# Transposing an 8192 x 8192 matrix: two load slots in place of three

## The chip, the cores and the metric

One core of a Trainium2 chip runs the kernel. The metric is the device time of one execution in microseconds (us); lower is better. Where several runs are shown, their median counts.

## The reference

```python
def setup_inputs():
    return {
        "x": np.random.randn(8192, 8192).astype(np.float32),
    }

def reference(x: np.ndarray) -> np.ndarray:
    return np.transpose(x)
```

The input and the output are 268 MB each, in HBM. Nothing is calculated; every element has to be read once, brought to another place and written once.

## The kernel before, in words

**Chunks.** The input is cut into chunks of 128 rows and 4096 columns, 2 MB each. There are two column halves of 64 row blocks, so 128 chunks; chunk t is row block t mod 64 of half t div 64. One step of the kernel is one chunk. A load (L100) brings a chunk into one of three slots `ins` of 16 KB per partition: chunk t goes to slot t mod 3.

**TensorE.** `transposes` (L109) waits until the slot's load has landed, and then transposes the chunk in 32 pieces of 128 x 128 through a multiplication with `ident` (L117), eight to each of four groups of PSUM banks. After each group it raises `s_pe` (L122). The loop of L132 runs on TensorE alone: its body is three steps, the slots 2, 0, 1, and slot 2 is skipped in the first turn, since 128 is not a multiple of three.

**Evictions.** Group h of a step (h = 0 to 3) is copied from PSUM to SBUF by ScalarE if h is even and by VectorE if it is odd (L208), once `s_pe` says that TensorE has done with it. A group holds two strips q = 2h and 2h + 1 of 512 columns each. A strip gathers eight consecutive chunks in a region of SBUF, 2 MB, before it is stored, so that rows of up to 1024 elements (4 KB) are written to the output. There are nine regions for the eight strips; a strip that begins a new region takes the one that has been free longest, and its eviction waits until that region's last store has landed (L189).

**Stores.** The strips are staggered: strip q is complete in steps with t mod 8 = q. So each step issues one store of 2 MB, after the eviction that completes it, which is in group h = (t mod 8) div 2: the first group in steps 0 and 1 of eight, the fourth in steps 6 and 7. At the beginning the regions hold fewer chunks and the stores are smaller (256 KB for the first), at the end all eight strips are stored in the last step. Where a strip runs over from one column half to the other, its store is split in two.

**Order.** All stores (L28, L160) and all loads but the first ones are issued by ScalarE's queue, ACT. Its program is written out step by step: the step's two evictions, the store at the place where the strip closes, then a wait until TensorE has done with the whole chunk (L223), then the load of the chunk that will use the same slot (L224). So the DMA queue of ACT receives stores and loads in turn. The first loads, one for each slot, are issued by SyncE (SP) at once. SP's last work is to wait for all stores (L226).

Of the kernel before, what the change touches and what calls it, by code (L numbers as in the profile page):

```python
# [40 lines left out]
def kernel(  # L41
# [12 lines left out]
    nc = tc.nc  # L54
    P = 128
# [5 lines left out]
    B = 4  # L61
    W = 8
    NR = S // B
    NIN = 3
    NREG = 9
    CH = N // P
    J = S * P

    with tc.tile_critical():  # L69
        nc.alloc_sbuf_tensor("pad", [P, 32], dt)  # L70
        ident = nc.alloc_sbuf_tensor("ident", [P, P], dt).ap()
        ins = [nc.alloc_sbuf_tensor(f"in{k}", [P, J], dt).ap() for k in range(NIN)]
        SIZE = B * W * P
# [3 lines left out]
        s_id = nc.alloc_semaphore("s_id")  # L77
        s_ld = [nc.alloc_semaphore(f"s_ld{k}") for k in range(NIN)]
        s_st = [nc.alloc_semaphore(f"s_st{k}") for k in range(NREG)]
        s_bank = [nc.alloc_semaphore("s_banka"), nc.alloc_semaphore("s_bankv")]  # L80
        s_pe = nc.alloc_semaphore("s_pe")
        s_cp = [nc.alloc_semaphore("s_cpa"), nc.alloc_semaphore("s_cpv")]

# [3 lines left out]
            out=ident,  # L87
            in_=ident,
# [6 lines left out]

        chunks = [(s, c) for s in range(M // J) for c in range(CH)]

        def load(t):
            s, c = chunks[t]
            (nc.sync if t < NIN else nc.scalar).dma_start(  # L100
                out=ins[t % NIN], in_=x[c * P:(c + 1) * P, s * J:(s + 1) * J]
            ).then_inc(s_ld[t % NIN], 16)

# [3 lines left out]
        def transposes(k):  # L109
            nc.tensor.sem_inc(s_ld[k], -16).wait_op(s_ld[k], 16, "sem-ge")  # L110
            for h in range(NR // 2):
                if h < 2:
                    n = NR // 4
                    nc.tensor.sem_inc(s_bank[h], -n).wait_op(s_bank[h], n, "sem-ge")  # L114
                for b in range(2 * B):
                    j = (2 * h + b // B) * B * P + b % B
                    tr = nc.tensor.transpose(  # L117
                        pss[h][:, b * P:(b + 1) * P],
                        ins[k][:, j:j + B * P - B + 1:B],
                        ident,  # L120
                    )
                tr.then_inc(s_pe, 1)  # L122

        T = len(chunks)
        assert T % NIN == NIN - 1
        pe = [nc.tensor.engine]
        for e in range(2):
            nc.tensor.sem_inc(s_bank[e], NR // 4)  # L130
        nc.tensor.wait_ge(s_id, 2)
        with nc.Fori(0, T // NIN + 1, engines=pe) as turn:  # L132
            with nc.tensor.If(turn > 0):
                transposes(NIN - 1)
            for k in range(NIN - 1):
                transposes(k)

        for t in range(NIN):
            load(t)
# [6 lines left out]
        def store(q, e, count):  # L146
            t0, r, parts = window.pop(q)
            nc.scalar.wait_ge(s_cp[e], count)
            base = 0
            for s, a, z in parts:  # L150
                rows = (z - a) * P
                j0 = s * J + q * B * P
                dst = out[j0:j0 + B * P, a * P:a * P + rows]
                dst = dst.rearrange("(q b) i -> q b i", q=P)
                src = regs[:, r * SIZE + base:r * SIZE + base + B * rows]
                base += B * rows
                if any(stored):
                    st = wide_dma(nc, nc.scalar, "qActDynamicHW", dst, src)
                else:
                    st = nc.scalar.dma_start(  # L160
                        out=dst, in_=src.rearrange("q (b i) -> q b i", b=B)
                    )
                st.then_inc(s_st[r], 16)
                stored[r] += 1
            free.append(r)

        def closes(w, t):
            t0, r, parts = w
            return t + 1 == t0 + sum(z - a for _, a, z in parts)

        for t, (s, c) in enumerate(chunks):
            for h in range(NR // 2):
                e = h % 2
                eng = (nc.scalar, nc.vector)[e]

                place = []
                for q in (2 * h, 2 * h + 1):
                    if q not in window:

                        span = (q - c) % W + 1
                        r = free.pop(0)
                        parts = [(s, c, min(c + span, CH))]
                        if c + span > CH and t + span < T:
                            parts.append((s + 1, 0, c + span - CH))
                        window[q] = (t, r, parts)
                        if stored[r]:
                            eng.wait_ge(s_st[r], 16 * stored[r])  # L189
                    t0, r, parts = window[q]  # L190
                    k = [p[0] for p in parts].index(s)
                    base = r * SIZE + B * P * sum(z - a for _, a, z in parts[:k])
                    _, a, z = parts[k]
                    place.append((base + (c - a) * P, (z - a) * P))
                ends = [q for q in (2 * h, 2 * h + 1) if closes(window[q], t)]
                gap = place[1][0] - place[0][0]
                runs = [(0, 1)]
                if place[0][1] != place[1][1] or abs(gap) >= 2 ** 15:
                    runs = [(0,), (1,)]
                eng.wait_ge(s_pe, t * NR // 2 + h + 1)  # L200
                closing = []
                for u in runs:
                    off, dist = place[u[0]]
                    dims = [list(regs.ap[0]), [gap, len(u)], [dist, B], [1, P]]
                    o = bass.AP(regs.tensor, regs.offset + off, dims)
                    i = pss[h][:, u[0] * B * P:(u[-1] + 1) * B * P]
                    i = i.rearrange("p (l b i) -> p l b i", b=B, i=P)
                    cp = nc.scalar.copy(out=o, in_=i) if e == 0 else nc.vector.tensor_copy(out=o, in_=i)  # L208
                    mine = [q for q in ends if q - 2 * h in u]
                    if mine:  # L210
                        cp.then_inc(s_cp[e], 1)
                        copied[e] += 1
                        closing += [(q, e, copied[e]) for q in mine]
                    if u is runs[-1]:
                        if mine:
                            eng.wait_ge(s_cp[e], copied[e])
                            eng.sem_inc(s_bank[e], 1)
                        else:
                            cp.then_inc(s_bank[e], 1)
                for k in closing:  # L220
                    store(*k)
            if t + NIN < T:
                nc.scalar.wait_ge(s_pe, (t + 1) * NR // 2)  # L223
                load(t + NIN)  # L224
        for r in range(NREG):
# [31 lines left out]
```

## Time and profile before

| what | value |
|---|---|
| median of three runs | 1264.52 us (1263.98 to 1265.18) |
| the profiled execution's own time | 1265.02 us |
| its span, first to last instruction | 1262.9 us |
| TensorE busy with matmuls | 742.7 us (59%) |
| VectorE busy | 316.1 us (25%) |
| ScalarE busy | 263.0 us (21%) |
| bytes moved by DMA | 536.98 MB, mean 425 GB/s |
| packets of ACT's queue, share of all DMA bytes | 98.8% |
| mean granted TensorE clock | 0.749 |

The profile is one execution, taken by the hardware profiler. TensorE's busy time sums matmuls that overlap with weight loads, so it says little of how much TensorE could do[...]. "DMA" in the slices is the mean busy share of the core's 16 DMA engines. For an issue of a DMA the page gives the median time from issue to landing, which includes the time that the transfer stands in the queue. The granted clock tells how much TensorE was throttled; one step's 32 matmuls take between 4.1 us (full clock, at the beginning) and 6.7 us.

### The profile page before, as it was taken

Reading aid. Unit: us, or ns where it says so; the run is one execution under the profiler, and the core shown is the slowest. Engines: PE = TensorE matmul, PEld = TensorE weight load, DVE = VectorE, ACT = ScalarE, POOL = GpSimd, SP = SyncE. Lnnn points to the kernel's source line nnn. Section 1 sums busy time; section 2 is a strip of 40 time slices with the busy share of each in tenths; the row PEclk is TensorE's granted clock in tenths of the full one; section 3 lists DMA queues with packets and bytes.
Section 4 is the critical chain, followed back from the end, with each engine's and each line's share of the span. In section 5 each row is a group of like instructions: output and inputs, shape, how many; then the busy total and the mean of one; then the engine's idle time right before and its main releaser. Section 6 shows DMA issues by size and latency. Waiting matters only on the chain. (4 is left out here: it accounts for less than half of the span.)

```text
span 1262.9 us, 9961 instructions
## 1 busy us (share of the span) xinstructions
PE 742.7 (59%) x4096; PEld 721.8 (57%) x4096; DVE 316.1 (25%) x311; ACT 263.0 (21%) x321; POOL 0.7 (0%) x6
## 2 busy tenths in 40 slices
PE   6565565665566555655566655666565655656561
PEld 5565555665566555655565655656565645655561
DVE  3322222222222222222222222222222222222220
ACT  3212121222122211212221121121212211122120
POOL 0000000000000000000000000000000000000000
PEclk9967768677777777686766687777868687777865
DMA  9999999999999999999999999999999999999998
GB/s 381 429 430 420 429 431 428 430 429 431 428 430 430 431 428 429 430 430 430 426 425 414 429 430 429 430 430 430 428 430 430 431 428 430 430 430 429 430 427 339
DMA packets 39274, 536.98 MB, mean 425 GB/s; under 512 B 4320, under 2 KB 4832, under 8 KB 6240
## 3 DMA queue, kind: packets, MB, share of 16 engines
q10 hardware_dynamic: 38832, 530.60, 98.8%
q1 hardware_dynamic: 432, 6.29, 1.2%
q14 instruction: 9, 0.07, 0.0%
q8 instruction: 1, 0.02, 0.0%
HBM read 268.44 MB, written 268.44 MB: 425 GB/s over the span
## 5 line engine op out<-in xcount | busy, mean ns | idle before, releaser
L117 PE MATMUL ps<-ident,in 128*128 128x128 f32 x4096 | 742.7, 364 | 493.1 <-PEq L114 493.1
L117 PEld LDWEIGHTS ps<-ident,in 128*128 128x128 f32 x4096 | 721.8, 219 | 513.9 <-issue 513.6
L208 DVE COPY regs<-ps 128x1024 f32<-128x1024 f32 (+1 forms) x311 | 316.1, 1034 | 921.2 <-PE ps L117 704.5
L208 ACT COPY regs<-ps 128x1024 f32<-128x1024 f32 (+1 forms) x320 | 261.7, 843 | 973.6 <-PE ps L117 654.9
L208 ACT ACT_TABLE_LOAD x1 | 1.3, 1283 | 0.9 <-SPq L69 0.9
L86 POOL TENSOR_SCALAR_AFFINE_SELECT ident<-ident 128x128 f32<-128x128 f32 x1 | 0.3, 293 | 0.2 <-POOL ident L84 0.2
L84 POOL MEMSET ident<- 128x128 f32 x1 | 0.2, 204 | 0.5 <-SPq L69 0.5
L241 POOL MEMSET const-bfloat16-1.0<- 128x1 bf16 x1 | 0.1, 102 | 0.0
L241 POOL MEMSET const-uint8-127<- 128x1 uint8 x1 | 0.1, 102 | 0.0
L241 POOL MEMSET const-float32-0.0<- 128x1 f32 x1 | 0.1, 99 | 0.2 <-issue 0.2
L241 POOL MEMSET const-float32-1.0<- 128x1 f32 x1 | 0.1, 99 | 0.0
## 6 DMA issues: line engine op xcount, KB each, us to landing
in<-in_x_dram ACTq DMA_DIRECT2D x125, 2048.0 KB, 22.5
out_dram<-regs ACTq DMA_DIRECT2D x114, 2048.0 KB, 18.4
out_dram<-regs ACTq DMA_DIRECT2D x4, 1792.0 KB, 17.5
in<-in_x_dram SPq DMA_DIRECT2D x3, 2048.0 KB, 11.6
out_dram<-regs ACTq DMA_DIRECT2D x4, 1536.0 KB, 15.1
out_dram<-regs ACTq DMA_DIRECT2D x4, 1280.0 KB, 16.7
out_dram<-regs ACTq DMA_DIRECT2D x4, 1024.0 KB, 16.6
out_dram<-regs ACTq DMA_DIRECT2D x4, 768.0 KB, 16.4
```

The lines of the kernel that those rows point to most:

```text
L84: nc.gpsimd.memset(ident, 0.0).then_inc(s_id, 1)
L86: nc.gpsimd.affine_select(out=ident, in_=ident, compare_op=mybir.AluOpType.not_equal, fill=1.0, base=0, pattern=[[-1, P]], channel_multipl ...
L117: tr = nc.tensor.transpose(pss[h][:, b * P:(b + 1) * P], ins[k][:, j:j + B * P - B + 1:B], ident,)
L208: cp = nc.scalar.copy(out=o, in_=i) if e == 0 else nc.vector.tensor_copy(out=o, in_=i)
L241: nc = _bacc.Bacc("TRN2", target_bir_lowering=False, num_devices=1)
```

## The change

There are two slots in place of three, so chunk t goes to slot t mod 2, and the load that ACT issues after step t is that of chunk t + 2 in place of t + 3. SP issues two loads at the beginning in place of three. TensorE's loop has two steps in its body and runs 64 turns, with no branch in it. The 16 KB of SBUF per partition that the third slot held stay unused; the regions, the evictions and the stores are as before.

The first load into a slot that has been used, that of chunk 2, is issued in two halves of 2048 columns: the first half after TensorE has done with the first two groups of chunk 0, the second after all four. Both raise a semaphore of their own, `s_half`. VectorE waits for both after its evictions of chunk 1 and then raises the semaphore of slot 0 by 16, for which TensorE waits. From chunk 3 on loads are issued whole, at the place in ACT's program where they stood.

```diff
-    NIN = 3
+    NIN = 2
...
+        s_half = nc.alloc_semaphore("s_half")
...
-        def load(t):
+        def load(t, part=None):
             s, c = chunks[t]
+            j0, j1 = (0, J) if part is None else (part * J // 2, (part + 1) * J // 2)
             (nc.sync if t < NIN else nc.scalar).dma_start(
-                out=ins[t % NIN], in_=x[c * P:(c + 1) * P, s * J:(s + 1) * J]
-            ).then_inc(s_ld[t % NIN], 16)
+                out=ins[t % NIN][:, j0:j1], in_=x[c * P:(c + 1) * P, s * J + j0:s * J + j1]
+            ).then_inc(s_ld[t % NIN] if part is None else s_half, 16)
...
-        assert T % NIN == NIN - 1
-        pe = [nc.tensor.engine]
+        assert T % NIN == 0
...
-        with nc.Fori(0, T // NIN + 1, engines=pe) as turn:
-            with nc.tensor.If(turn > 0):
-                transposes(NIN - 1)
-            for k in range(NIN - 1):
+        with nc.Fori(0, T // NIN, engines=[nc.tensor.engine]):
+            for k in range(NIN):
                 transposes(k)
...
                 for k in closing:
                     store(*k)
-            if t + NIN < T:
+
+                if t == 0 and h % 2:
+                    nc.scalar.wait_ge(s_pe, h + 1)
+                    load(NIN, h // 2)
+            if t == NIN - 1:
+                nc.vector.wait_ge(s_half, 32)
+                nc.vector.sem_inc(s_ld[0], 16)
+            if 0 < t < T - NIN:
                 nc.scalar.wait_ge(s_pe, (t + 1) * NR // 2)
                 load(t + NIN)
```

## The prediction

> **What bounds the kernel now.** I read the page's slices first, then the waits, the DMA issues, the timeline of the last full rounds, and the table of stretches. The slices say which resource is full:
>
> ```profile
> DMA  9999999999999999999999999999999999999998
> GB/s 381 429 430 420 429 431 428 430 429 431 428 430 430 431 428 429 430 430 430 426 425 414 429 430 429 430 430 430 428 430 430 431 428 430 430 430 429 430 427 339
> ```
>
> The DMA engines are busy in every slice and move about 430 GB/s in nearly all of them. 536.9 MB at 430 GB/s is 1248.6 us of a span of 1262.9 us; the 14 us left are the first slice (381), the last (339) and small dips. So a change helps only by making a transfer faster or filling a hole, and hurts by opening a hole. The waits and issues say how far the queue is ahead:
>
> ```profile
> DVE regs L208 <- PE ps L117: 704.5, 201, 12.2
> PEld ps L117 <- issue: 513.6, 128, 8.4
> ACT regs L208 <- DMA out_dram<-regs: 260.3, 45, 9.2
> DVE regs L208 <- DMA out_dram<-regs: 214.8, 30, 7.9
> ...
> in<-in_x_dram ACTq DMA_DIRECT2D x125, 2048.0 KB, 22.5
> out_dram<-regs ACTq DMA_DIRECT2D x114, 2048.0 KB, 18.4
> ```
>
> TensorE waits 128 times, once per chunk, for a load (513.6 us; 4.0 us a chunk). The evictions wait for TensorE and, 75 times, for a store to free a region. A load lands 22.5 us after its issue though it takes 2.1 MB / 430 GB/s = 4.88 us: it stands behind three to four others in one queue. That cover is what the change spends. One round and what comes after it, steps 125 to 127 (5, 6 and 7 of their group of eight):
>
> ```profile
> 1209.66 6.27 PE L117 MATMUL ps<-ident,in 128*128 128x128 f32 x32 [3.70 <-PEq L114]
> ...
> 1219.42 6.47 PE L117 MATMUL ps<-ident,in 128*128 128x128 f32 x32 [3.50 <-PEq L114]
> ...
> 1225.93 1.22 DVE L208 COPY regs<-ps 128x1024 f32<-128x1024 f32 x1 [1.52 <-PE ps L117]
> 1227.19 0.55 ACTq L28 DMA_DIRECT2D out_dram<-regs  x1
> ```
>
> A step lasts 1219.42 - 1209.66 = 9.76 us, two transfers of 4.88. TensorE needs P = 6.47 us of it (5.2 to 6.7 over the run, with the clock). Last, whether all DMA engines are equally far:
>
> ```profile
> 120.00:640.00 520.00, 309.75 (x1696) 301.19 (x1696) 132.13 (x133) 108.06 (x128) 0.00 (x0) 0.75 1.01 429
> 640.00:690.00 50.00, 31.09 (x160) 30.28 (x160) 12.57 (x15) 10.31 (x13) 0.00 (x0) 0.67 1.01 417
> ...
> 1256.00:1258.00 2.00, 0.00 (x0) 0.00 (x0) 0.00 (x0) 0.00 (x0) 0.00 (x0) 0.50 0.49 208
> 1258.00:1262.00 4.00, 0.00 (x0) 0.00 (x0) 0.00 (x0) 0.00 (x0) 0.00 (x0) 0.50 0.10 41
> ```
>
> The last two numbers of a row are DMA share and GB/s. At the end most engines stop near 1256.7 us and one or two go on to 1261.2: the slowest is some 4.5 us behind. The landing records say the same of the middle: the last of a load's 16 engines lands 3.6 us after the first at 300 us and 5.5 us at 1100 us.
>
> **What the Trainium skill says.** "DMA: Bandwidth & Descriptors", section Bandwidth, puts the ceiling at 435 GB/s (16 ports); the trace's 430 agrees, so no gain in rate is to be had. The same page, section Latency and other measured facts, gives about 0.6 us to the first byte for a DMA issued from SP or ACT; the trace has 1.0 us from the start of the first load's issue (0.94) to its first packet (1.94), with 0.37 us of issue in it. "Trainium Kernel Development and Optimization", Best Practices, asks for double buffering to overlap DMA with compute; the change is just that depth, and whether two are enough is the sum below.
>
> **Part 1: two slots, steady state.** Load t+2 is now issued when TensorE has done with chunk t; before, it was load t+3. The queue's order becomes load t, store t-1, load t+1, store t, load t+2. Count from L, when load t lands on the slowest engine. The landing comes about 0.4 us after the last packet (load 0: packets end at 7.54 to 7.83, landings 7.85 to 8.17). After L the queue still holds store t-1 and load t+1: cover to L + 9.76 - 0.4 = L + 9.36.
> What must arrive by then is store t. It comes latest in steps 6 and 7 of eight, where it follows the fourth eviction: load 126 lands at 1219.13 (0.29 ahead of the matmuls), the store is issued at 1227.19, L + 8.06 = P + 1.59. From issue to first packet take 1.3 us: at 1227.19 some engines had run dry and their next packets begin at 1228.4 to 1228.6. So the need is P + 2.9, met while P is below 6.46. The larger P of each of the 16 pairs of steps 6 and 7 is between 5.56 and 6.68; four exceed 6.46, by 0.02, 0.19, 0.03 and 0.22. A hole in step 6 lengthens the cover of step 7, so a pair counts once: +0.5 us. Other end: if the first packet pays the latency that load 0's first packets showed (1.36 against 611 ns, 0.75 more), the bound is P below 5.71 and the same sum over the pairs is 6.8 us; low end 0. I take 0.5, since the packets after the dry spot took the usual 611 ns.
> In the other six steps the store is issued at L + 3.4 to about L + 6.8, and the load after it at P + 0.3 (L + 6.8 at most), behind that store's 4.88 us: nothing.
>
> **Part 2: the engines lose their lead.** A fast engine now runs at most 9.36 - (P + 2.9), about 0 to 0.9 us, ahead of the slowest before it has nothing to do. Before, it could lead by 5 us, so a stall of one engine was absorbed when another was already behind. Summing in the DMA records the packets that took longer than usual, engine by engine: from step 20 on the worst engine loses 3.6 us (the landings: load 20 at 181.11 to load 127 at 1228.89 is 1047.8, less 107 x 9.76 = 1044.3, 3.5 us). With the leads cut back to the slack at each pair, the same stalls sum to about 6.0 us; with no slack at all, and the ramp in it, 10 us more than now. I take +2.5; ends 0 and +10.
>
> **Part 3: the ramp, and the two halves.** Two loads on SP's queue (2 x 0.4 us of issue) end at about 12.6 us in place of three at 17.7. The first half of load 2 is issued once TensorE has done half of chunk 0 (second eviction's start, 12.15), the second after 14.6. Store 0 (11.06 + 1.3 = 12.4) fills in until about 13.4, the first half arrives at 13.2 to 13.9 and takes 2.4 us, the second is there before it ends: a hole of 0 to 0.5. On ACT each half's issue (0.36) stands ahead of an eviction that waits for TensorE anyhow. The new wait on VectorE stands after chunk 1's evictions (end 20.5); nothing is queued behind it but chunk 2's, and TensorE waits for it: chunk 2 starts at about 20.8 against 19.48. Load 3 is issued at 19.2 and flows at 20.2 to 20.6, store 1 having ended at 20.0: another 0.2 to 0.6. From then on a load (4.88) and a growing store cover P of 4.1 us. Against this, the before kernel loses time here too (391 GB/s between 20 and 26 us, 0.5 us). Ends -0.8 and +1.5; I take +0.5.
>
> **Part 4: at nothing.** TensorE's loop has 64 turns of two steps, in place of 43 of three with a branch; its back edge falls into the 3.3 to 4 us wait for a load (without that cover I see 0.3 us between chunks 1 and 2). The 75 waits for stores (475 us) go: store t-1 lands at L + 4.9, and step t+1, which needs its region, starts at L + 9.76. What is late next there is TensorE, and behind it the load, so nothing is won. In the tail the first two final stores arrive at L + 4.7 with cover to L + 4.5: +0.2; the last bytes are the same.
>
> **Sum.** 0.5 + 2.5 + 0.5 + 0.2 = +3.7 us. The profiled execution took 1265.02 (span 1262.9 and 2.1 around it), so 1268.7 there; the median of the runs is 0.5 lower, 1264.52, so 1268.2.
>
> **The rivals.** *No change to be measured* (within 0.2%, 2.5 us, about what a measurement of this kernel tells from none): stalls seldom hit different engines and the slack holds; parts 1, 2 and 3 at 0.5, 0.5 and 0, about 1265.5. For it: the cover, 9.36, exceeds the need in 12 of 16 pairs.
> *Starved in steps 6 and 7*: the store pays full start latency and the engines go in lockstep. Parts at 5, 6 and 1: about 1276.5, up to 1284. It decides from a lead above 1.3 us. Against it: the packets at 1228.5, which were of normal length.
> *Faster*: the shallower queue ends the clog where stores are split at the middle of the run. There ACT's load issues take 3 to 5 us, the queue having no room, and the rate is 417: 13/430 x 50 = 1.5 us; with the 0.5 at 20 to 26 us and the 0.65 at 104 to 109 (374 GB/s in 5 us), and engines no more behind, -3.5 with nothing lost: 1261. It decides if the rate at that stage reaches 429 and stays 430 elsewhere. Against it: the same slow packets appear at 104 us, where nothing is clogged.
>
> **How the numbers follow.** Forecast (1267 to 1272) 0.45, no change 0.27, starved 0.18, faster 0.10. Range 1263 to 1278: it leaves out most of the faster case and the upper part of the starved one. Slower is 0.45 + 0.18.
>
> **What would show it.** Loads landing about 12 to 13 us after issue, stores near 8 to 10; no evictions waiting for stores; steps of 9.76 us with longer ones where P is above 6.46; DMA share below 1.0 only around steps 6 and 7; a last slice nearer 430, the engines ending together. A step of 10 us or more throughout steps 6 and 7 would make part 1 wrong; a rate above 430, or loads still 20 us in the queue, would overturn all of it.

## The result, and the profile after

| | before | after |
|---|---|---|
| time, median | 1264.06 us (1263.41 to 1265.18, 6 runs) | 1325.52 us (1318.0 to 1332.45, 6 runs) |
| ratio | | 1.0487, 95% interval 1.0442 to 1.0533 |
| profiled execution, own time / span | 1265.02 / 1262.9 us | 1318.0 / 1316.2 us |

The changed kernel is slower by 4.9%, some 61 us, where 3.7 us were forecast and the range ended at 1278. The sign was right, the size was not. The profiled execution of the changed kernel is the fastest of its six, so its trace shows 53 of the 61 us. The slices of the page and its DMA issues, of the changed kernel:

```profile
DMA  8999999999999999999999999999999999999999
GB/s 339 373 403 422 391 427 417 409 425 385 423 392 410 426 414 425 393 415 422 379 420 411 383 417 392 427 424 414 427 396 424 410 410 427 409 427 406 403 426 377
...
in<-in_x_dram ACTq DMA_DIRECT2D x125, 2048.0 KB, 13.5
out_dram<-regs ACTq DMA_DIRECT2D x114, 2048.0 KB, 9.6
```

The DMA engines still read "busy" in nearly every slice, but no slice reaches 430 GB/s and many lie at 380 to 415. So the busy digit hides the loss: the engines have work, and each piece of it takes longer. Landings come 13.5 and 9.6 us after issue in place of the 22.5 and 18.4 us of before. The waits (total us, times, longest us):

```profile
ACT regs L205 <- PE ps L119: 1006.8, 247, 9.1
DVE regs L205 <- PE ps L119: 977.6, 256, 12.2
PEld ps L119 <- issue: 571.5, 128, 8.6
```

The 75 waits of evictions for stores are gone, as forecast, and TensorE waits 571.5 us for loads, 58 us more than before. Cutting both traces where chunk 8's matmuls start (75.35 us, before 63.00) and where TensorE ends says in which stage the time went. The stretches (start and end; length; busy time and count of PE, PEld, DVE, ACT, POOL; clock, DMA share, GB/s), first of before, then of after:

```profile
0.00:63.00 63.00, 36.70 (x257) 35.17 (x257) 20.31 (x27) 18.34 (x31) 0.70 (x6) 0.97 0.98 405
63.00:1236.00 1173.00, 706.03 (x3840) 686.64 (x3840) 294.49 (x283) 243.58 (x288) 0.00 (x0) 0.74 1.01 429
1236.00:1263.00 27.00, 0.00 (x0) 0.00 (x0) 1.27 (x2) 1.07 (x2) 0.00 (x0) 0.55 0.78 324
```

```profile
0.00:75.35 75.35, 39.60 (x256) 38.19 (x257) 20.30 (x27) 18.34 (x31) 0.70 (x6) 0.87 0.94 355
75.35:1293.00 1217.65, 702.38 (x3839) 683.19 (x3840) 295.49 (x282) 244.91 (x288) 0.00 (x0) 0.75 1.00 412
1293.00:1316.00 23.00, 0.29 (x3) 0.10 (x1) 1.29 (x2) 1.07 (x2) 0.00 (x0) 0.55 0.94 390
```

The ramp costs 12.4 us, the 120 steps of the body 45.1 us (10.15 us each in place of 9.77), and the tail gives 4.1 us back: 53.3 us, the difference of the two spans (these figures take TensorE's exact ends, 1235.87 and 1293.29 us; the rows are cut at round times). In the body TensorE's work is the same, the DMA share is 1.00, and the rate is 412 GB/s and not 429. What it looks like from close by, in steps 6 and 7 of a group of eight (chunks 62 and 63), first the timeline (start, length, engine, line, operation; the wait before it in brackets), then stretches of 2 us:

```profile
626.45 5.46 PE L119 MATMUL ps<-ident,in 128*128 128x128 f32 x32 [5.62 <-PEq L116]
...
631.94 1.29 DVE L205 COPY regs<-ps 128x512 f32<-128x512 f32 x2 [0.63 <-PE ps L119]
632.66 0.55 ACTq L28 DMA_DIRECT2D out_dram<-regs  x1
633.25 0.60 ACTq L102 DMA_DIRECT2D in<-in_x_dram  x1
...
636.38 5.56 PE L119 MATMUL ps<-ident,in 128*128 128x128 f32 x32 [4.48 <-PEq L116]
```

```profile
630.00:632.00 2.00, 1.90 (x16) 1.71 (x15) 1.35 (x3) 0.98 (x2) 0.00 (x0) 1.00 1.03 442
632.00:634.00 2.00, 0.00 (x0) 0.00 (x0) 1.23 (x2) 0.10 (x1) 0.00 (x0) 1.00 0.67 287
634.00:636.00 2.00, 0.00 (x0) 0.00 (x0) 0.00 (x0) 0.00 (x0) 0.00 (x0) 1.00 0.96 401
636.00:638.00 2.00, 1.62 (x8) 1.65 (x9) 0.00 (x0) 0.00 (x0) 0.00 (x0) 0.64 1.01 393
638.00:640.00 2.00, 2.00 (x12) 2.00 (x11) 0.00 (x0) 1.07 (x2) 0.00 (x0) 0.51 0.94 279
```

The store is issued at 632.66, 6.5 us behind the landing of its chunk (626.16), when only the load that lands at 636.09 is ahead of it. Most of the engines are through with that load at about 633.1 us and have nothing until 633.9 (share 0.67). That is the hole that the forecast priced. But at 638 to 640 us the share is 0.94 and the rate 279 GB/s: hardly an engine is idle, the packets are long (up to 1.2 us, usually 0.611). Summing the DMA records from 80 us to 10 us before TensorE's end, averaged over the 16 engines: idle 10.0 us (before 0.2), time by which packets ran over their usual length 41.6 us (before 2.5). Four fifths of the loss have no hole at all.

A word on a quantity used below. *Lead* is the landing of the transfer ahead in the queue less the start of the issue, from the DMA records between 100 and 1200 us. *Lag* is how much later the last of the 16 engines lands than the median one. A landing counts for a semaphore only when all 16 engines are through (the Trainium skill, "DMA: Bandwidth & Descriptors", section Why a DMA increments its semaphore by 16 and not by 1, says that the engines finish independently); the traces agree, with a mean lag of 0.8 us in the changed kernel and 3.6 us in the kernel before. An engine that is ahead has that much less lead than the landings show.

### The profile page after: what moved, and what is told of

Its sections match the earlier page's. It is cut to its first block, busy times and chain, and to the rows that moved or that the text cites. A ratio compares the mean times of both kernels' runs of the same rounds, so it can differ in the third digit from the quotient of the medians.

```text
span 1316.2 us, 9919 instructions
## 1 busy us (share of the span) xinstructions
PE 742.3 (56%) x4096; PEld 721.5 (55%) x4096; DVE 317.1 (24%) x311; ACT 264.3 (20%) x321; POOL 0.7 (0%) x6
## 5 line engine op out<-in xcount | busy, mean ns | idle before, releaser
L119 PEld LDWEIGHTS ps<-ident,in 128*128 128x128 f32 x4096 | 721.5, 220 | 571.6 <-issue 571.5
## 6 DMA issues: line engine op xcount, KB each, us to landing
in<-in_x_dram ACTq DMA_DIRECT2D x125, 2048.0 KB, 13.5
```

The source lines that it names most:

```text
L119: tr = nc.tensor.transpose(pss[h][:, b * P:(b + 1) * P], ins[k][:, j:j + B * P - B + 1:B], ident,)
```

## The experiments

Times are medians; ratios are to the kernel before on the same chip, with 95% intervals, and are worked out from all runs, so they are not the quotients of two medians.

**Which part of the change costs.** *e1* gives the kernel before, with its three slots, loop and whole loads, the issue of the changed one:

```diff
-            if t + NIN < T:
+            if NIN <= t + 2 < T:
                 nc.scalar.wait_ge(s_pe, (t + 1) * NR // 2)
-                load(t + NIN)
+                load(t + 2)
```

> The kernel before, with its three slots, its loop of three and its whole first loads, but each load issued one step later (load t+2 after step t). Theory A (how far ahead loads are issued is what costs): as slow as the changed kernel or nearly, 1305 to 1330 us, steps of 10.2 us in the mean. Rival B (the slots themselves, TensorE's loop of two or the halves cost it): 1262 to 1272 us.

Measured: 1327.95 us, 1.0505 (1.0478 to 1.0532). *e2* is the changed kernel with load 2 issued whole and without VectorE's wait:

```diff
-                if t == 0 and h % 2:
-                    nc.scalar.wait_ge(s_pe, h + 1)
-                    load(NIN, h // 2)
-            if t == NIN - 1:
-                nc.vector.wait_ge(s_half, 32)
-                nc.vector.sem_inc(s_ld[0], 16)
-            if 0 < t < T - NIN:
+            if t < T - NIN:
```

> The changed kernel with load 2 issued whole after chunk 0, without halves and without VectorE's wait. Theory A: 1318 to 1330 us, the ramp within 4 us of the changed kernel's. Rival B2 (the halves and VectorE's wait cost the ramp its 8 to 12 us): 1308 to 1318 us.

Measured: 1325.53 us, 1.0469 (1.0442 to 1.0495). The later issue alone gives the whole loss; the number of slots, TensorE's loop and the halves of load 2 neither cost nor win anything that can be told.

**Is it ACT's queue?** *e3* is e2 with all loads issued by SP; *e8* is the kernel before with all loads issued by SP:

```diff
-            (nc.sync if t < NIN else nc.scalar).dma_start(
+            nc.sync.dma_start(
...
-                nc.scalar.wait_ge(s_pe, (t + 1) * NR // 2)
+                nc.sync.wait_ge(s_pe, (t + 1) * NR // 2)
```

> The kernel of e2_whole with every load issued by SP, in its own queue, once TensorE has done with the chunk; loads no longer stand behind a store in one queue. Theory A1 (a queue feeds its transfers one after the other, and a load right behind a store must be issued some 6.5 us ahead): the stretched packets go, 1264 to 1285 us. Rival C (two outstanding loads are too few bytes whatever the queue, or lockstep of the DMA engines costs it): 1310 us or more.

> The kernel before, three slots, with every load issued by SP in its own queue. Theory A2: 1261 to 1268 us, the lead is ample on either queue. Rival E (loads and stores side by side on two queues cost by themselves, as store and load on two queues took 13.1 us against 11.9 on one): 1280 us or more, and then the 1302 us of e3_sp tell nothing of the lead.

Measured: e3 1302.27 us, 1.0294 (1.0277 to 1.0312); e8 1274.84 us, 1.0058 (1.0039 to 1.0076). Over a third of e2's loss goes, most of it stays; at 1302 us, between the two expectations, e3 didn't decide. e8's 20 runs fall into two groups, 1265.8 to 1269.3 (9 runs) and 1274.3 to 1278.0 us; the profiled one is of the upper, and of its 11 us some 8 lie in the ramp (chunk 8 at 71.1 us), 1.5 in the body (9.79 us a step). "Trainium Kernel Development and Optimization" in the Trainium skill (section Key Constraints) says that a second issuing queue only saves issue time; e8's body agrees. With two slots it won 23 us (e3 against e2); whether by the earlier issue or by the second queue is not shown.

**How much earlier must a load be?** *e5*: the kernel before, load t + 2 issued after half of chunk t. *e7*: the changed kernel with every load in two halves, each with its own semaphore and issued when that half of the slot is free.

```diff
-            if t + NIN < T:
-                nc.scalar.wait_ge(s_pe, (t + 1) * NR // 2)
-                load(t + NIN)
+                if h == 1 and NIN <= t + 2 < T:
+                    nc.scalar.wait_ge(s_pe, t * NR // 2 + h + 1)
+                    load(t + 2)
```

> The kernel before with its three slots, but each load issued half a step late: load t+2 after the second eviction of step t (before: after the end of step t-1; e1_depth: after the end of step t). Theory A2: the lead stays above 6.5 us at every turn, so 1263 to 1275 us. Rival (the loss goes in proportion to the lead given up): about 1295 us.

```diff
+                if t + NIN < T and h % 2:
+                    nc.scalar.wait_ge(s_pe, t * NR // 2 + h + 1)
+                    load(t + NIN, h // 2)
```

> The changed kernel with every load in two halves with semaphores of their own, the first issued after half of the chunk, so half of each load comes some 3 us earlier. Theory A2: about half of the loss is won back, 1280 to 1305 us. Rival (two slots cost what they cost, whenever loads are issued): 1318 us or more.

Measured: e5 1293.45 us, 1.0215 (1.0179 to 1.0251); e7 1291.76 us, 1.0218 (1.0197 to 1.0239). Half the delay, about half the loss: I took this as "in proportion to what is outstanding", too soon, as e9 to e12 show. e7 has no ramp loss left (chunk 8 at 61.7 us), and still loses 0.2 us a step.

**Transfers by themselves.** *m1* issues groups of 2 MB stores (S) and loads (L) from an empty queue, *m2* groups of four and then alternating streams with 2, 3, 4 and 6 outstanding. The stream of m2, with `landed` waiting for the oldest one:

```python
        for depth in (2, 3, 4, 6):
            flying = []
            for n in range(24):
                if len(flying) == depth:
                    landed(*flying.pop(0))
                flying.append(issue("SL"[n % 2]))
```

> No transposing: only transfers of 2 MB in groups, each group issued into empty queues after the last has landed: a load; a store; store and load; load and store; two stores; two loads; store on ACT's queue with load on SP's; store, load, store, load. Theory A1: a store alone lands after 6.5 us (1.2 + 4.9 + 0.4), but with a load issued behind it on the same queue it lands after about 8 and the load after 13.5; on two queues both are there after 11.5. Rival C: store and load on one queue land after 6.5 and 11.4, as by bytes, and two queues change nothing.

> No transposing: transfers of 2 MB on ACT's queue. Groups issued at once into an empty queue: three stores and a load, three loads and a store; then alternating stores and loads, 24 of them with at most 2, then 3, 4 and 6 outstanding. Theory A2 (a load must be issued well ahead of the end of the store before it, and a store before the end of the load; then the turn costs nothing): the groups' last transfer lands after 21.1 and 21.7 us, as by bytes; the alternating ones take over 5.4 us each with 2 outstanding, about 5.1 with 3, 4.9 with 4 and 6. Rival D (each turn from writing to reading costs about 1 us when the 16 DMA engines make it together, however early it was issued): the groups take 22 to 23 us, and 4 or 6 outstanding still over 5.2 us each.

Measured in m1: a load alone lands 7.1 to 7.3 us after issue, a store 6.6. Store then load: the store takes 7.6, 1.0 more; load then store: the load 8.5, 1.3 more; two of a kind: no more than their bytes. In m2's groups, issued at once, three stores and a load were through after 22.2 us, three loads and a store after 23.0 to 23.7: 0.9 us and at least 1.1 us more than at 4.9 us for each further transfer, though the last one was issued 15 us or more before its turn; that is what the rival of m2 had expected. But in m2 all streams take about 5.0 us for a transfer, whatever the depth, once under way. So in a running stream neither a turn between storing and loading nor two outstanding transfers are slow by themselves; both ideas fell in that simple form, and the extra time of the groups stays unexplained. I then held that a turn costs when a transfer is issued late, less than about 2.4 us before the engines get to it, since in the changed kernel the stores with less than that stretched the packets. *m3* sweeps it: two outstanding, the next issue delayed by 0 to 7 chained copies.

```diff
                     landed(*flying.pop(0))
+                    for _ in range(copies):
+                        nc.scalar.copy(out=spare[:, 512:], in_=spare[:, :512]).then_inc(s_d, 1)
+                        late[0] += 1
+                        nc.scalar.wait_ge(s_d, late[0])
```

> Nothing is transposed and the output holds zeros; only stores and loads of 2 MB run, alternating, two outstanding at a time, both issued by ScalarE. In eight segments of 18 transfers, each next issue comes later after the landing of the transfer two before it, by 0 to 7 chained 128x512 copies, so that the work still ahead in the queue at an issue (the lead) shrinks from about 5 us to nothing. Theory E (a transfer that is issued less than about 2.4 us before the engines get to it costs about 1 us at its turn, besides any idle time): about 5.0 us for each transfer while the lead is above 2.4 us, 5.5 to 6 us when it is near 1.5 us, that is before the engines run dry by the 1.3 us of issue to first packet. Rival of bytes and first packet alone (what the prediction took): 5.0 us flat down to a lead of 1.3 us, and from there one us more for each us of delay. Rival that the number of bytes outstanding counts in proportion: the time of a transfer rises from the first copy on.

Measured, us for each transfer at mean leads of 4.9, 4.4, 4.1, 3.6, 2.4, 2.1, 1.7 and 1.3 us: 4.91, 5.05, 5.41, 5.52, 5.06, 5.45, 5.61, 5.91. The cost begins far above 2.4 us, against my theory and against that of bytes and first packet; the third expectation comes nearest, but the time doesn't rise steadily, and has a dip at 2.4 us (taken up again below the table).

**Issue everything earlier, with two slots.** *t1*: the changed kernel, the group with the closing strip transposed and evicted first, so that every store goes out early. *t2*: every second matmul left out.

```diff
+        ORDER = [(0, 1, 2, 3), (1, 0, 3, 2), (2, 1, 0, 3), (3, 0, 1, 2)]
...
-            for h in range(NR // 2):
+            for pos, h in enumerate(ORDER[t % W // 2]):
...
-                eng.wait_ge(s_pe, t * NR // 2 + h + 1)
+                eng.wait_ge(s_pe, t * NR // 2 + pos + 1)
```

> The changed kernel, but TensorE's loop has eight steps and in each step the group with the strip that closes is transposed and evicted first, so that in every step the store is issued about 3.4 us after the load's landing, as early as it now is in the first two steps of eight; two slots and the issue of the load at TensorE's end stay. Theory E (late stores of the later steps let the engines run dry or nearly so, and each time two turns cost about 1 us): 1264 to 1285 us. Rival (two outstanding loads, or issuing the load a step later, are the cost by themselves): 1310 us or more.

```diff
-                for b in range(2 * B):
+                for b in range(1, 2 * B, 2):
```

> The changed kernel with every second transposing matmul left out, half of the work of TensorE; those parts of the output are zero, everything else (slots, halves, order, sizes and number of transfers) is as in the changed kernel. Stores and loads are so issued some 2 to 3 us earlier in each step. Theory E (lead over the queue's end): 1264 to 1280 us. Rival (two outstanding loads are too few, whenever they are issued within a step): 1310 us or more.

Measured: t1 1322.43 us, 1.047 (1.0435 to 1.0505); t2 1309.79 us, 1.0367 (1.035 to 1.0385). In t1 stores have 2 us more lead, the moments at which at least 12 of the 16 engines have nothing to do fall from ten to none, and nothing is won that can be told; t2 wins some 15 of 61 us, far from the 1264 to 1280 us of my theory, which fell. The trace of t1 shows why it was too simple: its engines stand further apart, the mean lag is 4.2 us in place of 0.8, and the engines ahead have no more lead than they had (to the landing on the median engine, stores have 2.3 us in t1 and 3.3 in the changed kernel, as medians). *t4* adds e7's halves to t1, with an order of groups that keeps the two of a half together:

> The changed kernel's two slots with everything issued as early as it can be: each load in two halves with a semaphore of its own, issued as soon as half of the chunk is transposed, and the strip that closes transposed, evicted and stored first. Theory L: stores come as early as in the version with early stores, loads 3 us earlier, so the engines that are ahead of the last one have 4 us of lead or more: 1264 to 1280 us. Rival (in proportion to what is outstanding, here about 3 transfers): 1285 to 1297 us.

Measured: 1302.49 us, 1.0286 (1.0226 to 1.0346), no better than e7 alone. The changed kernel, e2, t1, t2 and t4 have one thing in common that I hadn't seen yet: the store stands ahead of the step's load.

**Time or order?** *e9*, *e10* and *e11* have three slots. Load t + 2 is issued by ScalarE between its wait for a group of chunk t and its first copy, ahead of the step's store in every step. e9 waits for the first group (its edit is shown), e10 for the second, e11 for the third; e5 had waited for the same group as e10, but its load stands behind the store in the steps in which one of the first four strips closes, and so goes out a little later there.

```diff
                 eng.wait_ge(s_pe, t * NR // 2 + h + 1)
+                if h == 0 and NIN <= t + 2 < T:
+                    load(t + 2)
...
-            if t + NIN < T:
-                nc.scalar.wait_ge(s_pe, (t + 1) * NR // 2)
-                load(t + NIN)
```

> Three slots, whole loads and the loop of the kernel before; load t + 2 is issued by ScalarE between its wait for the first group of chunk t and its copy of it, about 2 us after the landing of chunk t: some 5 us later than in the kernel before and some 5 us earlier than with one step's delay. Theory L (about 4 us of lead at the engines that are ahead, here 7 us or more): 1264 to 1275 us. Rival (the cost goes in proportion to the transfers outstanding, 4.3 before and 2.3 after, here about 3.3): 1285 to 1297 us.

> As the version that issues load t + 2 between ScalarE's wait and its copy of the first group of chunk t (same time as before, 0.9999), but that wait is now for the second group of the chunk, so the load goes out some 1.6 us later, at about the time of the version that gave 1.0215, and still ahead of the chunk's store in every step. Theory L (time of issue counts: the lead falls under what is needed): 1275 to 1297 us, 1.01 to 1.025. Rival (the order counts: the version with 1.0215 lost because load and store changed places from step to step): 1264 to 1268 us.

> The same with the wait for the third group of the chunk, another 1.6 us later, about 1.7 us earlier than with one step's delay (1.0505). Theory L: 1293 to 1325 us, between 1.0215 and 1.0505. Rival (order counts): 1264 to 1275 us.

Measured: e9 1264.35 us, 0.9999 (0.9991 to 1.0008); e10 1264.92 us, 1.0012 (0.9998 to 1.0025); e11 1269.52 us, 1.004 (1.0025 to 1.0054), all of it in the ramp, its body taking 9.77 us a step. The rival won: waiting for the same group, the order makes 1.0012 or 1.0215. The issues of e11, whose loads land nearly as soon after issue as the changed kernel's (13.5 us), while its stores stand nearly as deep as those of before (18.4):

```profile
in<-in_x_dram ACTq DMA_DIRECT2D x125, 2048.0 KB, 14.2
out_dram<-regs ACTq DMA_DIRECT2D x114, 2048.0 KB, 17.5
```

Two sets of DMA streams ran beside them:

> Again no transposing and zeros as output, only 2 MB stores and loads on ScalarE's queue, 24 in each segment; d is the number of chained 128x512 copies (0.66 us each) between a landing and the next issue. Stores and loads alternating, two outstanding, d = 0, 1, 2, 3, 4, 6; alternating, three outstanding, d = 7, 8, 9, 10, 11, 13 (which leaves about the lead of two outstanding with d = 0 to 6, since one more transfer of 4.9 us lies ahead); stores alone, two outstanding, d = 2, 3, 6; loads alone, the same. Theory L (what counts is the lead in us at the engines that are ahead of the last one, and it has to be about 4 us, where the first packet takes 1.3 us): 4.9 us for each transfer at d = 0 and at three outstanding with d = 7; 5.2 to 5.9 us from d = 2 and from d = 9 on, in the same way for both depths. Rival (the number of transfers outstanding counts): all segments of three outstanding 4.9 to 5.0 us up to d = 10. Whether turns between store and load are needed for the cost: if they are, stores alone and loads alone stay at 4.9 us up to d = 3; if they aren't, they rise as the alternating ones.

> No transposing, zeros as output; only 2 MB stores and loads on ScalarE's queue, 40 in each segment, with d copies of 0.66 us between a landing and the next issue. Alternating: two outstanding d = 0, 3; three outstanding d = 0, 2, 4, 6; four outstanding d = 0, 4. Loads alone: two outstanding d = 0, 1; three outstanding d = 0, 3, 6. Stores alone: two outstanding d = 4, 5; three outstanding d = 6. Before this, loads alone with two outstanding took 5.4 us each at a lead of 4.1 us, stores alone 4.91 down to 2.9 us. Theory L (lead in us, more of it for a load than for a store): three and four outstanding at a lead above 5.5 us take 4.9 us whatever d is; stores take 4.9 us down to a lead of 2 us. Rival (number outstanding): three outstanding 4.9 us for all d, two outstanding above 5.0 us for loads even at d = 0. The two differ where three outstanding have d = 6 (lead about 5.8 us) only if the needed lead is above that: then it is more than 5.0 us there.

m4's streams of three outstanding told nothing from eight copies on, which take ScalarE longer than a transfer, so that it was the bound; with seven a transfer took 5.16 us at a lead of 4.9, as with two outstanding at about that lead (5.10 at 5.1). The rest: stores alone 4.91 us each at a lead of 2.9 us and 5.31 at 1.4; loads alone 5.42 at 4.1. m5: alternating, two outstanding, 5.11 at 5.1 us of lead and 5.42 at 3.4; three outstanding 4.95 to 4.96 from 9.9 to 7.3 us and 5.02 at 6.1; four 4.95. Loads alone took 4.87 at 4.2 us, against m4's 5.42: by this count of the lead, what a load needs isn't settled.

**The order alone.** *e12* is the changed kernel, two slots, halves and all, with the stores of a step issued after its load:

```diff
         for t, (s, c) in enumerate(chunks):
+            waiting = []
...
-                for k in closing:
-                    store(*k)
+                waiting += closing
...
             if 0 < t < T - NIN:
                 nc.scalar.wait_ge(s_pe, (t + 1) * NR // 2)
                 load(t + NIN)
+            for k in waiting:
+                store(*k)
```

> The changed kernel, with one thing different: the stores of a step are issued after the step's load and not before it. Theory O (what costs is that the store goes ahead of the load, so that at its issue only one load is left ahead of it; behind the load its lead grows from about 4.7 to 11 us or more, as in the three slot versions with the load first, 1.0012 and 1.004): 1260 to 1280 us, although two slots, halves and the loop of two steps stay. Rival S (two slots and an issue at TensorE's end are too late in either order): 1300 us or more. The profile should show stores landing 16 us or more after their issue in place of 9.6, steps of 9.8 us, and evictions waiting for stores again.

Measured: 1272.31 us, 1.0071 (1.0057 to 1.0085). Its issues, its waits and its three stages (cut as above):

```profile
in<-in_x_dram ACTq DMA_DIRECT2D x125, 2048.0 KB, 13.4
out_dram<-regs ACTq DMA_DIRECT2D x114, 2048.0 KB, 17.5
```

```profile
ACT regs L206 <- DMA out_dram<-regs: 279.7, 50, 9.6
DVE regs L206 <- DMA out_dram<-regs: 213.3, 30, 8.0
```

```profile
0.00:72.24 72.24, 42.15 (x257) 40.76 (x257) 20.28 (x27) 18.34 (x31) 0.70 (x6) 0.88 0.95 359
72.24:1242.60 1170.36, 701.45 (x3840) 682.05 (x3840) 294.43 (x282) 244.56 (x290) 0.00 (x0) 0.75 1.01 428
1242.60:1269.50 26.90, 0.00 (x0) 0.00 (x0) 1.29 (x2) 0.02 (x1) 0.00 (x0) 0.55 0.86 358
```

The loads are issued as late as in the changed kernel and land after the same 13.4 us. The stores, which now wait for the load's issue, stand 17.5 us in the queue, and the body is back at 428 GB/s. The waits for stores are back too, 80 of them, 493 us, and cost nothing. What remains is the ramp (chunk 8 at 72.2 us, 9.2 later than before). So of the changed kernel's 61 us the order is worth 53 (1325.5 less 1272.3), the ramp about 8.

Side by side, from the profiled executions; lead as median and as the value that one in ten falls below:

| kernel | order in a step | lead of loads, us | lead of stores, us | lag, us | us per step | ratio |
|---|---|---|---|---|---|---|
| before | S, L (of t + 3) | 17.7, 16.2 | 13.4, 11.8 | 3.6 | 9.77 | 1 |
| e9 | L, S | 12.4, 9.7 | 13.4, 12.1 | 2.6 | 9.77 | 0.9999 |
| e10 | L, S | 10.7, 9.7 | 13.3, 12.3 | 3.6 | 9.78 | 1.0012 |
| e11 | L, S | 9.7, 9.0 | 13.0, 11.4 | 3.6 | 9.77 | 1.004 |
| e12 | L, S | 8.6, 7.9 | 12.7, 12.3 | 3.4 | 9.75 | 1.0071 |
| e5 | changing | 10.7, 5.9 | 9.4, 5.1 | 2.9 | 10.01 | 1.0215 |
| t4 | S among half loads | 12.9, 10.7 | 7.7, 6.4 | 4.2 | 10.07 | 1.0286 |
| t2 | S, L | 10.5, 9.3 | 6.2, 4.9 | 3.1 | 10.10 | 1.0367 |
| t1 | S, L | 8.4, 8.1 | 6.8, 6.2 | 4.2 | 10.21 | 1.047 |
| after | S, L | 8.5, 7.3 | 4.7, 2.8 | 0.8 | 10.15 | 1.0487 |

The loads of e12 and of the changed kernel have the same lead. The stores' lead (the value that one in ten falls below), less the lag, parts the table: 7.8 us and more in the upper five, 1.9 to 2.2 in the lower five. e1 has 1.6 and e7 3.0 in the same count; by the means of kernels nothing lies between 3.0 and 7.8 on one queue.

Single transfers tell more. Count the lead of each store only up to the landing of the transfer ahead on the *median* engine, and take the 101 steps of the changed kernel's own trace, between 100 and 1200 us, in which the store stands between two loads. The last column is the time by which the store's packets ran over their usual length, averaged over the engines (packets that start between the median landing of the transfer ahead and its own, each less 0.5 us):

| lead of the store on the median engine, us | stores | packets too long, us for each store |
|---|---|---|
| below 1 | 7 | 0.81 |
| 1 to 2 | 10 | 0.66 |
| 2 to 3 | 33 | 0.20 |
| 3 and more | 51 | 0.01 |

The traces of e1 and t2 fall off at the same place (0.21 and 0.24 us between 2 and 3, 0.01 from 3 on); in t1, where 94 of 100 stores have less than 3 us, all positions of the eight lose. None of the upper five kernels of the table has a store with less than 5 us in this count. So one kernel has full and slow stores side by side, and the line lies near 3 us. The same count puts the streams in order: the loads alone of m4 and m5, 5.42 and 4.87 us at nearly the same lead by landings, have 2.4 and 3.9 us on the median engine; two outstanding took 4.91 us at 4.5 (m3), 5.11 at 3.4 (m5), and the dip of m3 (5.06) has 2.1 us for its loads where its neighbours have 1.3 and 1.1. This was read from the traces afterwards; no run was made to try it.

## Why the prediction was wrong

**Why the order moves so much.** Count what is in the queue when load t lands. Before: store t - 2, load t + 1, store t - 1, load t + 2, four transfers, 19.5 us. Changed: store t - 1 and load t + 1, two, 9.8 us; both the third load and a store went with the third slot, because the store of step t goes out in the same step as the load behind it. Swapped: store t - 2, load t + 1, store t - 1, three, 14.6 us, and load t + 2 goes in ahead of store t. With the issue 3.4 to 8 us after the landing this gives stores a lead of 11 to 16, of 2 to 6, and of about 12 us, which the table has. The extra store keeps its region longer, which is why evictions wait for stores again in e12.

**Part 1** (+0.5 us, other end 6.8) is the step that failed. The queue, the cover of L + 9.36 and the store at P + 1.59 were right: stores land 9.6 us after issue (8 to 10 forecast), loads 13.5 (12 to 13), TensorE starts 0.3 us after a landing. Wrong was the test "need P + 2.9, met while P is below 6.46": that a store is in time if its first packet, 1.3 us after issue, arrives before the last landing's engine has run dry. The runs show packets of the usual length only from about 3 us on the median engine, and the price of less isn't the shortfall but slow packets: 41.6 us of them to 10.0 us of idling.

The 41 stores that had between 1.3 and 3 us, in time by the test, cost with the loads behind them 21.2 us in long packets and 0.8 us of idling. The place was right in the main: of the 46 us of long packets and idling in those 101 steps, 31 belong to the stores of steps 6 and 7 and the loads behind them. But "in the other six steps: nothing" failed: steps 4 and 5 have 9 us, the rest 5.5, and no position in the group of eight has a mean step below 9.90 us. Its own mark ("a step of 10 us or more throughout steps 6 and 7") was met in part: from step 6 to 7 the mean is 9.98 us, from 7 to the next group 10.30, and the one after that, whose load stands behind the store of step 7, 10.82. What misled it was the dry spot at 1228.5 us, whose packets took the usual 611 ns: it lies at the end of the run, with no load behind the store, and in m1 a store with nothing behind it takes 6.6 us and one with a load behind it 7.6. The body lost 45.1 us, where parts 1 and 2 had 3.0. As for the double buffering that the Trainium skill asks for ("Trainium Kernel Development and Optimization", Best Practices): two slots were enough for the body in the order load, store (9.75 us a step), and not in the order store, load.

**Part 2** (+2.5) had the right thing in view: the engines did lose their lead (lag 0.8 in place of 3.6 us). It priced that with each engine's own stalls, measured where the queue was deep. What the missing depth itself does to packets was not in the trace of before, so its upper end, 10 us, was no bound. How much of the 10.0 us of idling is this part's is not separated.

**Part 3** (+0.5, end +1.5). The halves cost nothing, as said (e2). The ramp's holes were mis-sized: 9.2 us at chunk 8 in e12, 12.4 in the changed kernel. Three of the stretches of 5 us of the changed kernel:

```profile
10.00:15.00 5.00, 4.71 (x32) 4.55 (x31) 2.16 (x4) 2.15 (x4) 0.00 (x0) 1.00 0.88 305
15.00:20.00 5.00, 3.71 (x29) 3.37 (x28) 2.96 (x5) 2.15 (x4) 0.00 (x0) 1.00 0.99 320
...
40.00:45.00 5.00, 3.91 (x23) 3.75 (x22) 2.46 (x3) 1.59 (x4) 0.00 (x0) 0.74 0.71 305
```

Against 430 GB/s these three lack 1.5, 1.3 and 1.5 us. At 40 us the engines are empty (0.71), while the stores are still small; "from then on a load and a growing store cover P" came true only later. At 15 us they are full and slow, in part because the stores are small: before moved 396 GB/s at a share of 1.00 between 14 and 20 us. So the ramp, +0.5 us in the forecast, measured +12.4. That every load in halves (e7) takes the loss away shows that it is the late issue.

**Part 4** held: TensorE's loop hides, nothing was won by the waits for stores that went. But they were read as a cost with cover and not as what they were, the mark of stores standing deep in the queue; in e12 they return with the speed. The tail came out at -4.1 us where +0.2 was said, since the engines end together (last slice 377 against 339 GB/s).

**The rivals.** "Starved in steps 6 and 7" was nearest, with its point ("from a lead above 1.3 us"), but put at 1276 to 1284 us and at two steps of eight, where two thirds of the body's loss was. "Faster" had against it what came: no slice above 430.

**What stays open.** Why packets take up to twice their time when the next transfer comes late, though still before the engines run dry. The line near 3 us on the median engine is that of stores between loads; stores alone kept 4.92 us a transfer down to 2.0 (m5), and for loads it lies somewhere between 2.4 and 3.9 in the streams. The groups of m2, which lost about 1 us at a turn issued early, don't fit it.

## What to carry over

Where one queue feeds a saturated DMA, count what stands ahead of each issue at the time of the issue, for stores as well as loads, and count it on the median engine, since the last one lags: here stores between loads kept their packets short with 3 us or more and lost with less, with the engines shown as busy in both. When a slot has to go, look at the order in the program first: issuing the load ahead of the store gave back 53 of 61 us in the changed kernel. And evictions that wait for stores can be the sign of a queue that is deep enough, not of one that is too slow: 75 of them before and 80 in e12, none in the changed kernel.

## What the runs showed of the hardware that was not expected

- A busy share of 0.94 to 1.00 with 279 to 412 GB/s: packets of 16 KB that often take 0.9 to 1.2 us in place of 0.611 when the next transfer comes late.
- A store issued 3 us or more before the median engine was through with the load ahead had packets of the usual length (0.01 us over), one with 1 to 2 us ran 0.66 us over, with hardly an engine idle.
- From an empty queue a store with a load right behind it takes 1.0 us longer, a load with a store behind it 1.3 us; two of a kind take no longer.
- The last DMA engine lags the median by 2.6 to 4.2 us in the kernels of the table (before 3.6, t1 4.2), except the changed one (0.8), whose engines idled for 10 us.
